# Values of all heads by seven half-size products, five of them in front of head 0, with weight sums and low parts made by accumulating DMAs

## The chip, the core and the metric

One NeuronCore of a Trainium2 chip runs the whole program. The metric is device time in microseconds; the median of the runs counts. PE is TensorE, DVE VectorE, ACT ScalarE, POOL GpSimd, SP the engine that only issues transfers.

## The reference, cut to what matters

A trunk of two layers on 512 tokens of 1024 features. Layer 0 mixes tokens by pooling, layer 1 by differential attention with 8 heads; each is followed by a SwiGLU network, and each sum by a layer norm. The change is in the attention, whose values are one product of (512 x 1024) by (1024 x 1024):

```python
qkv = x @ w_qkv
q, k, v = jnp.split(qkv, 3, axis=-1)
...
s = jnp.einsum('bhcqd,bhckd->bhcqk', q[:, :, :, q0:kend], k[:, :, :, :kend]).astype(jnp.float32) * sm_scale
...
p = jax.nn.softmax(s, axis=-1)
a = p[:, :, 0] - lam * p[:, :, 1]
outs.append(jnp.einsum('bhqk,bhkv->bhqv', a.astype(v.dtype), v[:, :, :kend]))
...
o = o * lax.rsqrt(jnp.mean(jnp.square(o), axis=-1, keepdims=True) + LN_EPS)
```

## The kernel before

Every float32 operand is split into two float32r parts: a high part, which ACT makes by a cast, and a low part, source minus high, which DVE (or POOL) makes by a subtraction. `mm3` (L125) multiplies high by high, high by low and low by high into one bank of PSUM, so each product costs three matmuls. There are eight banks of 128 x 512.

All weights lie in `wall`, in rows of 128 x 1024 (512 KB) in the order of their use. `fetch` lets SP load the next row into one of five raw buffers (`RAWS`), `ready` splits the next row into one of six pairs (`WBUFS`), `take` in the attention gives out the next pairs. A load waits until the buffer five rows back is free. The order of instructions on each engine is the order of the program text: nothing is rearranged, and an instruction that waits holds back all that stand behind it on its engine.

`xt` holds x transposed and split, in two halves of 256 tokens. `transposed` (L210) lets PE turn a block of 128 tokens into two banks, `turned` (L219) lets ACT apply gamma and beta from there, and splits the result into `xt`. Blocks are called 0 to 3. At the end of the first SwiGLU network block 2 is turned in `ffn`, and block 3 by `late` in the middle of head 0.

Attention, for each head h, in this order on PE: the values (two heads of 128 columns are made together for two blocks of tokens, 48 matmuls of 256 columns for each h), the sum of squares of head h-2 (`root`), the queries (24 matmuls of 512 columns), the ten transposes of the weights of head h-1, the keys (24), `mix` of head h-1 with the values (12), and the scores of head h in four blocks (24). Behind the scores DVE adds the bias and takes the row minimum, ACT makes the exponentials, DVE combines the two maps (`combine`); behind `mix` ACT squares and casts (sq, sqh), POOL makes the low part (sql), which `root` multiplies by ones. In heads 1 to 4 DVE also applies gamma and beta to one block of the residual (`affine`). The bias of the next head is loaded by SP one head ahead. Head 0 has no values of an earlier head to mix: its queries and keys are made in two halves of tokens, 96 matmuls of 256 columns, because block 3 is late.

The down projection of `ffn` already uses seven products in place of eight (`DOWN`, `multiply`, L886): two halves of tokens, two halves of the inner dimension, two halves of the columns. There sums of weight quarters are made by accumulating DMAs that POOL issues (`load_terms`, L664 to 666).

Of the kernel before, what the change touches and what calls it, by code (L numbers as in the profile page):

```python
# [54 lines left out]
def trunk(ctx, tc, x, wall, pscale, lam_p, subln, table, lng, lnb, band, first, onehot, out):  # L55
# [37 lines left out]
    total = wall.shape[0]  # L93

    def fetch(upto):
        while fetched[0] < min(upto, total):
            c = fetched[0]
            raws[c] = keep.tile([P, 1024], F32, tag="raw", name=f"raw{c}", bufs=RAWS)
            nc.sync.dma_start(out=raws[c], in_=wall[c])
            fetched[0] += 1  # L100
# [11 lines left out]
    def ready(upto, low=None):  # L112
        while divided[0] < min(upto, total):
            c = divided[0]
            fetch(c + RAWS)
            h, l = weight_pair(f"w{c}")
            split(h, l, raws.pop(c), low=low)
            parts[c] = (h, l)
            divided[0] += 1
# [99 lines left out]
    def turned(n, s):  # L219
        for i, pt in enumerate(turns.pop((n, s))):  # L220
            y = keep.tile([P, 4, P], F32, tag="y", name=f"y{n}_{s}_{i}", bufs=2)
# [12 lines left out]
    def turn(n, s):  # L234
        transposed(n, s)
        turned(n, s)

# [225 lines left out]
    def ffn(layer, late):  # L463
# [5 lines left out]
        with tc.tile_pool(name=f"ffn{layer}", bufs=1) as fp:  # L469
# [392 lines left out]
            load_gb(n)  # L862
# [33 lines left out]
            for p in DOWN:  # L896
# [18 lines left out]
                for s in range(2):  # L915
# [15 lines left out]
                    elif p == "Q4":  # L931
# [17 lines left out]
                        if not final:  # L949
                            turn(n, 1 + s)  # L950
                            ready(c1 + FB + 3 + s)
# [3 lines left out]
    def attention(late):  # L955
        n = 2
        with tc.tile_pool(name="attn", bufs=1) as ap:
# [10 lines left out]
            ah = ap.tile([P, AW], F32R, name="ah")  # L968
            al = ap.tile([P, AW], F32R, name="al")
            for t in (ah, al):  # L970
                nc.gpsimd.memset(t[:, :P].bitcast(F32), 0.0)
# [20 lines left out]
            whole = region("heads").rearrange("p (h i t) -> p h i t", h=HEADS, i=2)  # L992
# [11 lines left out]
            vs, vw, qk, soft, outs, mid, biases = {}, {}, {}, {}, {}, {}, {}  # L1004

            started = {}

            def start_values(h, j):
                c, i = h // 2, h % 2
                if c not in vw:  # L1010
                    vw[c] = take(2)
                if j == 0:
                    started[h] = bank(f"v{h}")
                s = 2 * i + j
                for k in range(KB):
                    wh, wl = vw[c][k // 4]
                    o = (k % 4) * 256
                    mm3(
                        started[h][:, j * 256 : (j + 1) * 256],
                        x_at(k, s * P, (s + 1) * P),  # L1020
                        (wh[:, o : o + 256], wl[:, o : o + 256]),
                        k == 0,
                        k == KB - 1,
                    )

            def values(h):
                for j in range(2):
                    if j or h not in started:
                        start_values(h, j)
                vh = ap.tile([P, 2, 256], F32R, tag="vh", name=f"vh{h}", bufs=3)  # L1030
                vl = ap.tile([P, 2, 256], F32R, tag="vl", name=f"vl{h}", bufs=3)
                return vh, vl, started.pop(h)

            def split_values(h, v):
                vh, vl, acc = v
                split(vh.rearrange("p a b -> p (a b)"), vl.rearrange("p a b -> p (a b)"), acc)
                vs[h] = (vh, vl)

            def query(acc, w, lo, hi):
                wh, wl = w  # L1040
                for k in range(KB):
                    mm3(
                        wide(acc, lo, hi),
                        (wh[:, k * P : (k + 1) * P], wl[:, k * P : (k + 1) * P]),
                        x_at(k, lo, hi),
# [4 lines left out]
            def split_query(h, nm, acc):  # L1050
                hh, ll = (slots[6 if nm == "q" else 7][:, i, :] for i in range(2))
# [77 lines left out]
            def mix(h):  # L1129
                vo = (h % 2) * P  # L1130
                acc = bank(f"o{h}")
                for k in range(SB):
                    vh, vl = vs[2 * (h // 2) + k // 2]
# [3 lines left out]
                        (vh[:, k % 2, vo : vo + P], vl[:, k % 2, vo : vo + P]),  # L1137
# [43 lines left out]

            load_bias(0)
            for h in range(HEADS):
                v = values(h)
                if h > 0:
                    combine(h - 1, 3)
                ready(where[0] + 2)
                split_values(h, v)
# [12 lines left out]
                accs = [bank(f"{nm}{h}") for nm in "qk"]  # L1201
                w = take(2)
                if h == 0:
                    query(accs[0], w[0], 0, 256)
                    late()
                    query(accs[1], w[1], 0, 256)
                ready(where[0] + 1)
                query(accs[0], w[0], 256 if h == 0 else 0, 512)
                split_query(h, "q", accs[0])
                if h > 0:  # L1210
                    transposed(h - 1)
                query(accs[1], w[1], 256 if h == 0 else 0, 512)
                if h == 0:
                    split_query(h, "k", accs[1])
                    start_values(1, 0)
                ready(where[0] + 2)
                if h > 0:
                    split_query(h, "k", accs[1])
                ready(where[0] + 3)
                if h > 0:  # L1220
# [12 lines left out]
            combine(HEADS - 1, 3)  # L1233
            ws = take(4)
# [31 lines left out]
    attention(later(1, 3))  # L1266
# [31 lines left out]
def layout(w):  # L1298
# [32 lines left out]
    v = cols(qkv[:, 2 * D :], 256)  # L1331
    v = v.reshape(4, P, 2, 1024).transpose(0, 2, 1, 3)
    for h in range(HEADS):
        if h % 2 == 0:
            pieces.append(v[h // 2])
# [41 lines left out]
```

## Time and profile before

| | us |
|---|---|
| median of three runs | 949.88 (949.42 to 952.01) |
| span of the profiled execution | 947.3 |
| first value matmul of head 0 | 374.2 |
| first scores of head 0 | 395.9 |
| first scores of head 6 | 527.8 |
| end of the last head's scores | 552.4 |

In the rows of a timeline the columns are start, duration, engine, line, operation, output and inputs, form, number, and in brackets the idle time before it and who ended it. The rows of groups give busy time and the mean in ns. The rows of stages give, for each engine, busy time and number of instructions. "DMA to landing" is minimum, median and maximum from the issue to the arrival.

### The profile page before, as it was taken

Reading aid. Unit: us, or ns where it says so; the run is one execution under the profiler, and the core shown is the slowest. Engines: PE = TensorE matmul, PEld = TensorE weight load, DVE = VectorE, ACT = ScalarE, POOL = GpSimd, SP = SyncE. Lnnn points to the kernel's source line nnn. Section 1 sums busy time; section 2 is a strip of 40 time slices with the busy share of each in tenths; the row PEclk is TensorE's granted clock in tenths of the full one; section 3 lists DMA queues with packets and bytes.
Section 4 is the critical chain, followed back from the end, with each engine's and each line's share of the span. In section 5 each row is a group of like instructions: output and inputs, shape, how many; then the busy total and the mean of one; then the engine's idle time right before and its main releaser. Section 6 shows DMA issues by size and latency. Waiting matters only on the chain.

```text
span 947.3 us, 15363 instructions
## 1 busy us (share of the span) xinstructions
PE 934.1 (99%) x5976; PEld 845.7 (89%) x5976; DVE 781.3 (82%) x1149; ACT 490.1 (52%) x788; POOL 108.4 (11%) x133
## 2 busy tenths in 40 slices
PE   9999999999999999999999999999999999999996
PEld 8898899999988888988888888998899999988885
DVE  8859879999988777688777677789779999987778
ACT  6752444555564457655566553833345554564450
POOL 4121121110001101000000000211111110001101
PEclk9999999999999999999999999999999999999998
DMA  9387988885888964333233222396888885878952
GB/s 244 125 266 236 341 269 246 265 261 208 255 255 271 363 219 136 95 89 101 78 123 83 64 90 90 118 324 197 262 266 250 255 272 204 261 249 271 356 171 90
DMA packets 82248, 196.99 MB, mean 208 GB/s; under 512 B 14804, under 2 KB 26324, under 8 KB 82174
## 3 DMA queue, kind: packets, MB, share of 16 engines
q1 hardware_dynamic: 42876, 115.07, 36.9%
q0 software_dynamic: 15520, 46.14, 17.8%
q10 hardware_dynamic: 23778, 34.78, 10.2%
q8 instruction: 47, 0.77, 0.3%
q14 instruction: 27, 0.22, 0.1%
HBM read 159.25 MB, written 36.72 MB: 207 GB/s over the span
## 4 chain that ended last, share of the span: by engine, by line
PE 92%; DVE 4%; ACT 2%; issue 1%; POOL 0%; DVEq 0%; POOLq 0%
PE A L820 17%; PE P L886 13%; PE C L820 9%; PE Q L886 6%; PE B L820 4%; PE g L129 3%; PE u L128 3%; PE u L127 3%; PE u L129 3%; PE g L127 3%; PE g L128 3%; PE s L1085 2%; PE v L127 2%; PE v L128 2%; PE v L129 2%; PE q L128 2%
## 5 line engine op out<-in xcount | busy, mean ns | idle before, releaser
L566 DVE TENSOR_TENSOR raw<-raw,raw 128x1024 f32<-128x1024 f32 x56 | 68.3, 1219 | 0.5
L109 ACT CAST xs<-hid 128x512 fp32r<-128x512 f32 (+1 forms) x60 | 34.7, 581 | 24.4 <-DVE hid L734 24.4
L224 ACT ACTIVATE y<-pt,bT,gT 128x128 f32<-128x128 f32 x96 | 36.1, 456 | 20.1 <-PE pt L213 20.1
L110 DVE TENSOR_TENSOR xs<-hid,xs 128x512 fp32r<-128x512 f32 (+1 forms) x60 | 38.5, 644 | 7.8 <-ACT xs L109 7.8
L1095 ACT ACTIVATE p<-p,mn 128x128 f32<-128x128 f32 (+3 forms) x64 | 35.4, 554 | 14.9 <-DVE mn L1090 14.9
L665 POOL DMA_DIRECT2D b<-in_wall x20 | 14.0, 705 | 175.0 <-DVE g_58l L572 66.1
L598 DVE TENSOR_TENSOR hid<-sg,u 128x512 f32<-128x512 f32 x16 | 11.0, 687 | 27.5 <-PE u L129 16.8
L726 POOL DMA_DIRECT2D xs<-ssum x24 | 17.4, 725 | 140.7 <-PE Q L886 119.5
L177 POOL TENSOR_TENSOR rs<-rs,mhalf 128x1 f32<-128x1 f32 x16 | 12.5, 784 | 170.5 <-DVE rs L176 131.0
L110 DVE TENSOR_TENSOR xt<-y,xt 128x512 fp32r<-128x512 f32 x24 | 16.3, 689 | 17.5 <-ACT xt L109 17.5
L1090 DVE CUSTOM_DVE_ANT_0 p<-s,bias 128x128 f32<-128x128 f32 (+3 forms) x64 | 28.1, 485 | 0.0
L665 POOL DMA_DIRECT2D hid<-in_wall x24 | 18.7, 821 | 81.1 <-DMA tsum<-hid 49.4
L110 POOL TENSOR_TENSOR sql<-sq,sqh 128x512 fp32r<-128x512 f32 x7 | 9.0, 1291 | 165.3 <-ACT sqh L109 165.3
L702 ACT CAST v<-u 128x512 fp32r<-128x512 f32 x22 | 13.6, 620 | 26.9 <-DVE u L700 26.7
L168 DVE BATCH_NORM_STATS2 st<-res 128x6 f32<-128x512 f32 x32 | 22.2, 695 | 1.1
L846 ACT ACTIVATE sg<-sg 128x512 f32<-128x512 f32 x14 | 8.9, 633 | 25.7 <-DVE sg L839 25.7
L110 DVE TENSOR_TENSOR heads<-k,heads 128x512 fp32r<-128x512 f32 x8 | 5.5, 692 | 19.9 <-ACT heads L109 19.9
L614 ACT CAST xs<-hid 128x1024 fp32r<-128x1024 f32 x8 | 8.4, 1051 | 24.0 <-DVE hid L631 11.6
L666 POOL DMA_DIRECT2D hid<-in_wall x12 | 14.8, 1232 | 48.2 <-DMA hid<-in_wall 44.9
L835 DVE TENSOR_TENSOR hid<-C,hid 128x512 f32<-128x512 f32 x14 | 9.7, 692 | 10.8 <-PE C L820 9.2
L1109 DVE SCALAR_TENSOR_TENSOR p<-p,sm,p 128x128 f32<-128x128 f32 (+3 forms) x32 | 17.7, 552 | 1.1
L109 ACT CAST heads<-k 128x512 fp32r<-128x512 f32 x8 | 4.7, 589 | 26.0 <-PE k L129 26.0
(1119 smaller groups left out, 3727.7 us busy)
## 6 DMA issues: line engine op xcount, KB each, us to landing
raw<-in_wall SPq DMA_DIRECT2D x122, 512.0 KB, 4.5
r<-tsum SPq DMA_DIRECT2D x40, 512.0 KB, 4.3
hid<-in_wall POOLq DMA_DIRECT2D x36, 512.0 KB, 6.9
b<-in_wall POOLq DMA_DIRECT2D x30, 512.0 KB, 6.4
r<-in_wall SPq DMA_DIRECT2D x30, 512.0 KB, 4.5
tsum<-hid ACTq DMA_DIRECT2D x24, 512.0 KB, 5.3
ssum<-v ACTq DMA_DIRECT2D x22, 512.0 KB, 4.4
tsum<-b ACTq DMA_DIRECT2D x20, 512.0 KB, 5.2
```

The costliest lines, as they stand in the source:

```text
L109: nc.scalar.copy(dst_h, src)
L110: (low or nc.vector).tensor_tensor(dst_l, src, dst_h.bitcast(F32), op=ALU.subtract)
L127: nc.tensor.matmul(acc, ah, bh, start=start, stop=False)
L128: nc.tensor.matmul(acc, ah, bl, start=False, stop=False)
L129: nc.tensor.matmul(acc, al, bh, start=False, stop=stop)
L224: nc.scalar.activation(y[:, k, :], pt[:, k * P : (k + 1) * P], AF.Identity, bias=bT[:, n, kk : kk + 1], scale=gT[:, n, kk : kk + 1],)
L566: tt(t, raws[pair[0]], raws[pair[1]], op=ALU.add)
L665: nc.gpsimd.dma_start(out=t[:, j], in_=src[:, j])
L820: nc.tensor.matmul(o, w[:, c], x[:, kk, :], start=p in ("P1", "Q5", "P2") and f + kk + e == 0, stop=p in ("Q4", "Q3", "P2") and (f, kk, e) ...
L886: nc.tensor.matmul(accs[s], x[:, k, r], y[:, c], start=first and k == 0 and e == 0, stop=last and k == m - 1 and e == 2, skip_group_check= ...
L1090: nc.vector.tensor_tensor_reduce(out=p, in0=accs[c][:, :w], in1=biases[h][:, w - 1 :: -1] if w < S else biases[h][:, ::-1], op0=ALU.add, o ...
L1095: nc.scalar.activation(p, p, AF.Exp, bias=mn[:, q, c : c + 1], scale=-1.0, accum_out=sm[:, q, c : c + 1],)
```

## The change

The value weights are cut into quarters W11, W12, W22, W21 (first index: half of the inner dimension, second: half of the columns, two rows of `wall` each), and x into X11, X12 (tokens 0 to 255) and X21, X22. Seven products of (256 x 512) by (512 x 512) take the place of eight: P1 = X11 W11, P2 = X12 W21, P6, P7, Q4, Q5 and Q3 with sums of quarters on the left, on the right or on both. All values of all heads are kept in float32 in `vals` (16 KB per partition), and each head splits its 128 columns from there.

Five products (P1, P2, P6, P7, Q4) stand in front of head 0, with the queries and keys of head 0 (now 48 matmuls of 512 columns) between P2 and P6; Q5 and Q3 are in head 1. Heads 2 to 7 make no values. Blocks 2 and 3 are both turned in the attention, and their float32 form is kept (`kept`) for the sums over x, which DVE and ACT make as in `ffn`.

The right-hand sums are made by accumulating DMAs on POOL's queue: `tall` (in the place of gamma and beta, which are loaded later) is W11, then plus W12, plus W22, and after its first use plus W21; `short` is W12 plus W22; rows 6 and 7 are W11 plus W12 in the raw buffer. For 14 rows of queries and keys (8, 9 and 12 to 23 counted from the attention's first row) the low part is no longer a subtraction on DVE: ACT casts the high part, ACT writes its negative into the low part, and a DMA adds the row from memory to it.

```diff
+    order_of_rows = (
+        [vrow[0], vrow[0] + 1, vrow[3], vrow[3] + 1, qrow, qrow + 1, vrow[0], vrow[0] + 1]
+        + [qrow + 2, qrow + 3, vrow[2], vrow[2] + 1]
+        + list(range(qrow + 4, qrow + 2 * HEADS))
+    )
...
+    added = {attn + 6 + r: vrow[1] + r for r in range(2)}
+    by_dma = {attn + c for c in (8, 9, *range(12, 24))}
...
-            nc.sync.dma_start(out=raws[c], in_=wall[c])
+            nc.sync.dma_start(out=raws[c], in_=wall[rows_of_wall[c]])
+            if c in added:
+                nc.gpsimd.dma_start(out=raws[c], in_=wall[added[c]], accum_op=ALU.add)
...
+            if c in by_dma:
+                nc.scalar.copy(h, raw)
+                nc.scalar.mul(l, raw, -1.0)
+                nc.gpsimd.dma_start(
+                    out=l, in_=wall[rows_of_wall[c]].bitcast(F32R), accum_op=ALU.add
+                )
+            else:
+                split(h, l, raw, low=low)
...
+            nc.sync.dma_start(out=tall, in_=two_rows(0))
+            nc.sync.dma_start(out=short, in_=two_rows(1))
+            nc.gpsimd.dma_start(out=tall, in_=two_rows(1), accum_op=ALU.add)
+            nc.gpsimd.dma_start(out=short, in_=two_rows(2), accum_op=ALU.add)
+            nc.gpsimd.dma_start(out=tall, in_=two_rows(2), accum_op=ALU.add)
...
+            def values(p, r, accs, w):
+                wh, wl = w
+                xh, xl = (lefts[p][:, i] for i in range(2))
+                for s in range(2):
+                    t = slice(s * P, (s + 1) * P)
+                    for q in range(2):
+                        kk = 2 * r + q
+                        c = slice(q * 512, (q + 1) * 512)
+                        for e, (a, b) in enumerate(((xh, wh), (xh, wl), (xl, wh))):
+                            nc.tensor.matmul(
+                                accs[s], a[:, kk, t], b[:, c],
+                                start=p in ("P1", "Q5", "P2") and kk + e == 0,
...
+            flip(1, 2)
+            va = [bank(f"va{s}") for s in range(2)]
+            w = take(2)
+            for r in range(2):
+                values("P1", r, va, w[r])
+            flipped(1, 2, (r0, r1))
+            whole_x(r2, 0, 0)
+            flip(1, 3)
+            ready(where[0] + 3)
+            vb = [bank(f"vb{s}") for s in range(2)]
+            w = take(2)
+            for r in range(2):
+                values("P2", r, vb, w[r])
+            whole_x(r3, 0, 1)
+            flipped(1, 3, (r0, r1))
+            ready(where[0] + 2)
+            combined(r1, r0, r1, ALU.subtract)
+            combined(r0, r2, r0, ALU.subtract)
+            combined(r2, r1, r2, ALU.subtract)
+            accs = [bank(f"{nm}0") for nm in "qk"]
+            w = take(2)
+            query(accs[0], w[0])
+            high(3, r0)
+            high(0, r2)
+            for s in range(2):
+                nc.scalar.copy(part(0, 0, s), vb[s])
+            low(3, r0)
+            low(0, r2)
+            wide6 = [pair_of(f"vt{r}", tall[:, r]) for r in range(2)]
+            nc.gpsimd.dma_start(out=tall, in_=two_rows(3), accum_op=ALU.add)
+            for s in range(2):
+                combined(part(0, 0, s), va[s], part(0, 0, s), ALU.add)
+            split_query(0, "q", accs[0])
+            query(accs[1], w[1])
+            wide7 = [pair_of(f"vs{r}", short[:, r]) for r in range(2)]
+            for r in range(2):
+                values("P6", r, va, wide6[r])
+            split_query(0, "k", accs[1])
+            for s in range(2):
+                nc.scalar.copy(part(0, 1, s), va[s])
+            combined(r3, r3, r2, ALU.add)
+            high(1, r1)
+            high(2, r3)
+            for r in range(2):
+                values("P7", r, va, wide7[r])
+            low(1, r1)
+            wide4 = [pair_of(f"vu{r}", tall[:, r]) for r in range(2)]
+            for s in range(2):
+                nc.scalar.copy(part(1, 1, s), va[s])
+            low(2, r3)
+            load_gb(1)
+            for r in range(2):
+                values("Q4", r, va, wide4[r])
+            ready(where[0] + 4)
...
             load_bias(0)
             for h in range(HEADS):
-                v = values(h)
                 if h > 0:
                     combine(h - 1, 3)
-                ready(where[0] + 2)
-                split_values(h, v)
+                if h == 1:
+                    vc = [bank(f"vc{s}") for s in range(2)]
+                    w = take(2)
+                    for r in range(2):
+                        values("Q5", r, vc, w[r])
+                    ready(where[0] + 4)
+                    for s in range(2):
+                        combined(part(1, 1, s), vc[s], part(1, 1, s), ALU.subtract)
+                if h > 0:
+                    split_values(h - 1)
                 if h > 1:
                     root(h - 2)
...
+                    query(accs[1], w[1])
+                    ready(where[0] + 2)
                     split_query(h, "k", accs[1])
+                    if h == 1:
+                        w = take(2)
+                        for r in range(2):
+                            values("Q3", r, vc, w[r])
...
+                    ready(where[0] + 3)
                     mix(h - 1)
```

More of the change, by code (lines that the diff above doesn't have):

```diff
@@ L236, in turn @@
         turned(n, s)
+    flip, flipped = transposed, turned
     lines = dram.tile([HEADS, LINE], F32, name="lines")
@@ L1026, in values @@
[L1026 to L1036, printed above, removed]
+            vs, qk, soft, outs, mid, biases = {}, {}, {}, {}, {}, {}
@@ L1265, in trunk @@
     ffn(0, {(0, 1): later(0, 2), (1, 0): later(0, 3)})
-    attention(later(1, 3))
+    attention()
     ffn(1, {(0, 1): later(2, 3)})
```

148 lines of the change are left out of this document (90 added, 58 removed).

## The prediction

> **What bounds the kernel now.** I read the page's engine line, TensorE's waits, then busy time by stage.
>
> ```profile
> span 947.3 us, 15363 instructions
> PE 934.1 (99%) x5976; PEld 845.7 (89%) x5976; DVE 781.3 (82%) x1149; ACT 490.1 (52%) x788; POOL 108.4 (11%) x133
> PE q L128 <- DVE xt L110: 0.2, 1, 0.2
> 373.40:395.86 22.46, 22.29 (x184) 21.96 (x184) 13.76 (x25) 16.42 (x31) 1.00 (x4) 1.00 0.34 101
> 491.21:513.70 22.49, 22.49 (x145) 19.79 (x144) 15.13 (x39) 13.32 (x31) 1.29 (x1) 1.00 0.29 84
> ```
>
> The page gives PE 99%, and of the waits of all PE's matmuls the only one inside attention is the 0.2 us on xt. The two stage rows (from the first transpose of block 2 to the first scores; from the q of one head to the q of the next; columns PE, PEld, DVE, ACT, POOL, then granted clock) say that PE has no idle time there to give back, while ACT is busy 13.32 us and DVE 15.13 us of 22.49. So fewer matmul columns are worth their time, if nothing new makes PE wait; and a new wait costs its full length.
>
> **The saving.** First and last matmul of groups of 24 (256 and 512 columns), the instruction behind each, and twelve 512-column matmuls of the kind that the products will be (x stationary):
>
> ```profile
> 380.07 0.28 PE L127 MATMUL q<-xt,w70h 128*128 128x256 f32 x1
> 382.83 0.29 PE L129 MATMUL q<-xt,w70l 128*128 128x256 f32 x1
> 382.96 1.03 PE L213 MATMUL pt<-ident,res 128*128 128x128 f32 x8
> 383.75 0.36 PE L127 MATMUL k<-xt,w71h 128*128 128x256 f32 x1
> 491.21 0.40 PE L127 MATMUL q<-xt,w84h 128*128 128x512 f32 x1
> 496.66 1.25 PE L1120 MATMUL at<-ident,p 128*128 128x128 f32 x10
> 301.89 0.39 PE L886 MATMUL P<-d_14h,xs 128*128 128x512 f32 x1
> 304.61 0.39 PE L886 MATMUL P<-d_15h,xs 128*128 128x512 f32 x1
> ```
>
> 256 columns take (382.96-380.07)/24 = 0.120 us, 512 take 5.45/24 = 0.227, for x stationary 2.72/12 = 0.227. Values: 8 heads x 48 x 0.120 = 46.1 us now; 7 products x 24 x 0.227 = 38.1 after. Head 0's queries and keys: 96 x 0.120 = 11.5 becomes 48 x 0.227 = 10.9. **Saving 8.6 us**, all on the path. Transposes stay.
>
> **Front: weight sums against PE.** P6 needs W11, W12 and W22 added by two accumulating DMAs onto one tile, 1 MB each, one after the other. Rows: the SP queue, landings of the loads, of plain and of accumulating POOL loads (512 KB each), the best throughput, and one cast, subtraction and evacuation each:
>
> ```profile
> 373.40 1.09 PE L213 MATMUL pt<-ident,res 128*128 128x128 f32 x8 [0.16 <-DVE res L186]
> 375.85 0.33 SPq L99 DMA_DIRECT2D raw<-in_wall  x1
> 376.99 0.42 SPq L964 DMA_DIRECT2D gcol<-in_subln  x1
> 377.45 0.43 SPq L1058 DMA_DIRECT2D bias<-lines  x1
> DMA to landing us min/median/max: 3.5/4.2/4.9
> L665 POOL DMA_DIRECT2D hid<-in_wall x24: 722/739/1240, 46.4 to 744.2; - x24
> DMA to landing us min/median/max: 4.2/6.4/10.5
> L666 POOL DMA_DIRECT2D hid<-in_wall x12: 1222/1230/1243, 55.1 to 748.6; - x12
> DMA to landing us min/median/max: 5.8/6.9/10.8
> 22.00:24.00 2.00, 2.00 (x19) 2.00 (x18) 1.97 (x5) 0.00 (x0) 0.56 (x1) 1.00 1.04 426
> L109 ACT CAST w70h<-raw x1: 1042/1042/1042, 373.5 to 373.5; 128x1024 fp32r<-128x1024 f32 x1
> L110 DVE TENSOR_TENSOR w70l<-raw,w70h x1: 1226/1226/1226, 374.6 to 374.6; 128x1024 fp32r<-128x1024 f32 x1
> L110 DVE TENSOR_TENSOR vl<-v,vh 128x512 fp32r<-128x512 f32 x8 | 5.5, 684 | 0.0
> ```
>
> 512 KB at 426 GB/s is 1.2 us of data. Accumulating lands 1.6 later than plain at the least (5.8 against 4.2), so its data part is 2.8. No row shows 1 MB accumulating: I take 5.8+2.8 = 8.6; bounds below. The tile's first load takes the place of the bias load on SP, 377.45, and lands 4.2+1.2 later: 382.8. Two accumulations: 400.0. Then cast 1.04, two subtractions 2x1.23, and P1's sum must be read out of the bank that P6 goes on adding to (0.7): P6 can start at 404.2. PE gets there at 373.40 + 2x0.79 (transposes) + 4x5.45 (P1, P2, q, k) = 396.8. **Wait 7.4.** Low end: a megabyte at the price of 512 KB, 5.8: 1.8. High end: the accumulation onto the other tile stands between the two on POOL, and its 5.6 of data runs in front of the second by 2.5: 9.9. The accumulation of raw row 7 is ahead of them on POOL: it waits for SP's load of 375.85, 4.2 later 380.0, and takes 1.23, so it is through 1.5 us before the tile lands; if that cover goes, the wait grows by the same.
>
> One rule speaks against the change here. The Trainium skill ("SBUF — State Buffer", "Who interferes with whom") has DVE and GpSimd share a port pair that one locks for a whole instruction; POOL's descriptors can be held by DVE. Here plain issues of POOL took 739 ns in the median and 1240 at most beside a DVE that is 82% busy, so three issues could lose 1.5 us by these rows, 3.7 if each waited for one subtraction; I add nothing.
>
> Queued behind ACT's waiting cast are the split of head 0's q, the second half of the sum, the other tile's casts and k's split; PE asks for none of them before P7 or the scores. The sums over x (10 x 1.23 on DVE, 4 x 1.04 on ACT) I cost at nothing: P2, q and k hide them. Block 3's activations and splits lie in these rows, first and last:
>
> ```profile
> 383.59 1.51 ACT L224 ACTIVATE y<-pt,bT,gT 128x128 f32<-128x128 f32 x4 [0.75 <-PE pt L213]
> 387.85 0.69 DVE L110 TENSOR_TENSOR xt<-y,xt 128x512 fp32r<-128x512 f32 x1 [1.37 <-ACT xt L109]
> ```
>
> They took 5.0 us (to 388.54). Now the transposes end at 373.40+2x0.79+5.45 = 380.4, so 386.5 with one row split between, and five steps of 1.2 lead to the low half that P6 reads: 392.5, 4 us before PE. With that cover gone each further step costs 1.2.
>
> **Head 0's bias.** Its load stood at 377.45, 18 us early. Now it is on SP behind the gamma and beta load (held until the fourth sum of weights is split) and four raw loads, the last of which needs the buffer of row 8, free after two casts, a copy and a copy with the sign turned on ACT, 4 x 1.0, begun about with Q4.
>
> ```profile
> bias<-lines SPq DMA_DIRECT2D x8, 256.0 KB, 3.5
> ```
>
> Landing at Q4 start + 4.0 + 0.7 (issues) + 3.5 = 8.2, or up to 3.7 later for three of the loads. Q4 and the scores take 5.45+2.1; Q5 then needs banks that the scores fill until a first minimum (0.5): wait 1.1 to 4.8. I take 3.0; ends 0 (loads drained early) and 5.
>
> **Heads 2 to 7: less to cover with.** Before, 48 value matmuls (5.8 us) stood between the scores of a head and the sum of squares of the last. Scores 6 on PE, ACT, POOL, DVE:
>
> ```profile
> 526.42 1.05 ACT L109 CAST w92h<-raw 128x1024 fp32r<-128x1024 f32 x1
> 527.92 0.60 ACT L1145 ACTIVATE sq<-o 128x512 f32<-128x512 f32 x1 [0.45 <-PE o L129]
> 528.55 0.62 ACT L109 CAST sqh<-sq 128x512 fp32r<-128x512 f32 x1
> 529.25 1.29 POOL L110 TENSOR_TENSOR sql<-sq,sqh 128x512 fp32r<-128x512 f32 x1 [21.21 <-ACT sqh L109]
> 527.75 2.21 PE L1085 MATMUL s<-heads 64*128 64x256 f32 x24
> 529.89 0.38 PE L127 MATMUL v<-w86h,xt 128*128 128x256 f32 x1
> 536.18 0.75 DVE L1109 SCALAR_TENSOR_TENSOR p<-p,sm,p 128x512 f32<-128x512 f32 x1
> L205 DVE TENSOR_TENSOR res<-res,gb 128x1024 f32<-128x1024 f32 x8 | 9.8, 1219 | 0.0
> 490.98 0.40 PE L1153 MATMUL ss<-sql,ones 128*128 128x512 f32 x1
> ```
>
> sql ends at 530.54; PE is free at 529.89, and without values its next matmul reads sql: 0.65 of wait even in today's order. The row of weights behind k now takes two ACT passes instead of one: 1.0 more against 0.45 idle ahead of sq, so 0.6 later: **1.2 per head**. Second, the transposes need the last combination, done at 536.93 (+0.5 for the same ACT delay). PE reaches the one that needs it at 529.89 + 1.2 + 0.46 (ss) + 5.45 (q) + 0.3 = 537.3, so it hides most of this: 0.2 more. Six heads: 8.4. Floor: ACT not late, 0.7 each, 4.2. In heads 2 to 4 DVE also has the affine of one block (2 x 1.22) ahead of scaled and the q and a splits, with 5.8 us less to do it in; DVE's 15.13 less three row subtractions plus 2.4 is 13.9 of 16.7, in order, behind ACT: I estimate 1.2 per head, 3.6 (0 to 7.2). **Together 12.0** (4.2 to 15.6). The 14 subtractions taken from DVE (17 us) shorten nothing that PE waits for; the low parts that DMA completes are asked for 12 us later, against 5.8 to 6.9 of landing.
>
> Moving the gamma and beta load, raw sums of rows 6 and 7 and the reordered rows change no PE work; they were loaded a head early.
>
> **Sum.** -8.6 + 7.4 + 3.0 + 12.0 = +13.8: span 961.1. The median of the runs shown is 949.88, 2.6 above the span, so **963.7**. The ends: -8.6+1.8+0+4.2 = -2.6, 947.3; -8.6+9.9+5+15.6 = +21.9, 971.8.
>
> **Rivals.** (1) *The heads keep pace*, the other side: one mechanism, at the wait for sql and the last combination. If PE comes there no earlier than these (below 0.1 us a head), the 12.0 fall away: 951.7, no change. For it: the first minimum of scores 6 waited for a row subtraction that is gone. Against: 530.54 against 529.89, with today's ACT. (2) *The weight sums come early*, 5.8 a megabyte: 5.6 less, 958.1. (3) *All is hidden* but that 1.8: -6.8, 943.1; it needs both and the bias in time. (4) *The front is worse*: wait 9.9, and the clock falls in it, P6's 5.45 at half speed: 963.7+2.5+5.5 = 971.7.
>
> ```profile
> 935.00:940.00 5.00, 3.57 (x16) 2.63 (x14) 4.97 (x9) 0.00 (x0) 0.05 (x1) 1.00 0.39 145
> 940.00:947.00 7.00, 0.00 (x0) 0.00 (x0) 3.62 (x7) 0.00 (x0) 0.92 (x1) 0.56 0.33 123
> ```
>
> For (4): where PE stands still at the end, the granted clock is 0.56. The Trainium skill ("TensorE: Matmul & The Clock Gate", "Part 1: The HAM clock gate") says that a window of some 3.4 us idle halves the clock, and as long a busy one restores it: an estimate by that page is 1.7 us after a wait like P6's, in place of 5.5. No row in the middle of this kernel shows such a wait.
>
> **Numbers.** Forecast 0.52, (1) 0.14, (2) 0.14, (3) 0.12, (4) 0.08. A measurement tells 0.3% (2.8 us) from no change: faster is (3) and 0.02 of (1), 0.14; same 0.07 of (1); slower the rest, 0.79. Range 947 to 973, from the low end of the sum to just past (4): only (3) and some of (4) lie outside. The forecast alone: 957 to 970.
>
> **What would show it.** PE idle of 2 to 10 us at the first matmul of P6, released by DVE's reading of P1's banks, ACT's cast before it waiting for a DMA; PE idle at Q5 from minima that wait for the bias; in heads 2 to 7 PE idle of about 1 us at ss, released by POOL's sql; a head then lasts 18 to 20 us, not 22.5. Wrong if P6 follows k without a gap, or if ss follows the scores without one: then DMA or ACT is faster in place than the rows say.

## The result, and the profile after

| | before | after |
|---|---|---|
| median, us | 949.65 (949.25 to 952.01) | 980.50 (979.31 to 981.94) |
| span of the profiled execution, us | 947.3 | 979.3 |
| first scores of head 0 | 395.9 | 431.5 |
| first scores of head 1 | 415.2 | 471.5 |
| first scores of head 7 | 550.3 | 582.1 |

The ratio is 1.0325 (95% interval 1.0308 to 1.0342). The forecast was 963.7, its range ended at 973: the direction is right, the time is 16.8 us off. After the first scores of head 7 both kernels need the same, 397.0 and 397.2 us of span, so all of the loss lies in the attention ahead of it.

The engine line of the page after, columns as before:

```profile
span 979.3 us, 14929 instructions
PE 935.2 (96%) x5712; PEld 831.6 (85%) x5712; DVE 786.3 (80%) x1157; ACT 515.7 (53%) x820; POOL 127.3 (13%) x153
```

PE has 264 matmuls fewer and is yet busy 1.1 us longer, and its idle time grew from 13.2 to 44.1 us. Two causes show in the next two views: waits, and a lower clock. First the waits of PE's matmuls (engine, line, tile, who ended the wait; us in total, times, longest):

```profile
PE va L1067 <- DVE vals L1246: 15.1, 1, 15.1
PE vc L1067 <- DVE mn L1140: 9.8, 1, 9.8
PE ss L1202 <- POOL sql L124: 3.3, 6, 0.9
PE q L151 <- DMA w80l<-in_wall: 1.2, 1, 1.2
```

Before, the list had 0.2 us inside the attention. The first row is P6 waiting until DVE has read P1's sums, the second Q5 waiting until DVE's first minima free the banks of the scores. Then busy time by stage (PE, PEld, DVE, ACT, POOL, granted clock, DMA share, GB/s): from the transposes to the end of k, the wait, P6 in two pieces, the wait at Q5, Q5:

```profile
373.19:397.00 23.81, 23.79 (x112) 19.61 (x112) 18.86 (x22) 15.20 (x29) 4.43 (x6) 1.00 0.97 258
397.00:412.09 15.09, 0.00 (x0) 0.03 (x1) 3.11 (x4) 4.18 (x5) 1.63 (x2) 0.64 0.64 125
412.09:417.60 5.51, 5.51 (x13) 4.35 (x14) 5.05 (x6) 0.67 (x2) 0.74 (x1) 0.50 0.76 132
417.60:423.00 5.40, 5.40 (x24) 4.38 (x24) 0.75 (x1) 2.91 (x4) 0.00 (x0) 0.95 0.30 60
434.43:444.25 9.82, 0.00 (x1) 0.00 (x1) 0.63 (x5) 0.51 (x3) 0.00 (x0) 0.72 1.04 297
444.25:450.00 5.75, 5.75 (x16) 4.57 (x17) 5.49 (x23) 4.42 (x15) 0.00 (x0) 0.60 0.08 33
```

In the first stage PE is never idle, as forecast, but look at the DMA share: 0.97 of all sixteen DMA engines. In the kernel before it was 0.34 up to the first scores (a row of the prediction), and the forecast never added up what the change puts on top of that. After the wait PE runs at clock 0.50 for 5.5 us and does 13 matmuls where 24 would fit. P6 took 412.09 to 420.48, 8.4 us, in place of 5.45, and Q5 7.75: 2.9 and 2.3 us that are no wait in any list.

Where the 15.1 us come from, in the rows of the timeline around the weight sums (start, duration, engine, line, operation, what ended the idle time):

```profile
377.58 0.38 SPq L1004 DMA_DIRECT2D tall<-in_wall  x1
385.01 1.21 POOL L1006 DMA_DIRECT2D tall<-in_wall  x1 [3.02 <-DMA tall<-in_wall]
389.89 1.20 POOL L1007 DMA_DIRECT2D vals<-in_wall  x1 [3.67 <-DMA vals<-in_wall]
398.56 1.18 POOL L1008 DMA_DIRECT2D tall<-in_wall  x1 [7.48 <-DMA tall<-in_wall]
407.91 1.04 ACT L123 CAST vt0h<-tall 128x1024 fp32r<-128x1024 f32 x1 [15.17 <-DMA tall<-in_wall]
411.26 1.28 DVE L1246 TENSOR_TENSOR vals<-va,vals 128x512 f32<-128x512 f32 x2
412.09 0.77 PE L1067 MATMUL va<-vt0h,heads 128*128 128x512 f32 x1 [15.11 <-DVE vals L1246]
```

The chain is the forecast one, link by link: load, first accumulation, second accumulation, cast, DVE, P6. Its durations are not: the load took 7.4 us (forecast 5.4), the first accumulation 13.5 (8.6), the second 9.3 (8.6). The other tile, whose load stands behind it on SP and whose accumulation stands between on POOL, is in `vals` (that is where `short` lies).

What the DMA engines of the kernel after did from 376 to 410 us (queue, packets, MB, share of 16 engines; then issues with KB each and median us to landing):

```profile
q0 software_dynamic: 1042, 3.94, 58.8%
q1 hardware_dynamic: 1264, 3.80, 31.8%
...
tall<-in_wall POOLq DMA_DIRECT2D x2, 1024.0 KB, 11.2
...
vals<-in_wall POOLq DMA_DIRECT2D x1, 1024.0 KB, 13.1
```

The same two queues over the whole span of the kernel before:

```profile
q1 hardware_dynamic: 42876, 115.07, 36.9%
q0 software_dynamic: 15520, 46.14, 17.8%
```

0.588 x 34 us for 3.94 MB is 5.1 us of all sixteen engines per MB on POOL's queue, which carries the accumulations here; 0.318 x 34 for 3.80 MB is 2.8 us per MB on SP's queue of plain loads. Together that is 30.8 of 34 us, and the last sum that P6 needs is there at 407.9: until then the engines are full, and what is queued on them needs about the time that passes. Accumulating costs nearly twice the engine time of plain loading. The page of before had a hint: 0.178 x 947.3 / 46.14 = 3.65 us per MB on POOL's queue, where some transfers accumulate, against 3.04 on SP's. At those prices the same 3.94 and 3.80 MB make 25.9 us. Counted from 376, that estimate has the last sum at 402 and a wait of about 9 us at P6: nearer than the forecast, and still short.

The wait at Q5, rows of the timeline:

```profile
426.53 0.33 SPq L177 DMA_DIRECT2D gb<-in_lng  x1
...
431.06 1.01 SPq L1108 DMA_DIRECT2D bias<-lines  x2
...
443.89 0.29 DVE L1140 CUSTOM_DVE_ANT_0 p<-s,bias 128x128 f32<-128x128 f32 x1 [8.65 <-DMA bias<-lines]
444.25 0.80 PE L1067 MATMUL vc<-w74h,heads 128*128 128x512 f32 x1 [9.82 <-DVE mn L1140]
```

The bias is issued 5.1 us after Q4 began (forecast 4.7) and is read 12.8 us later (landing forecast at 3.5, at most 7.2): gamma and beta, four rows of weights and two low parts are on the same engines, whose share in the wait is 1.04.

The heads. Score to score (start of the first scores of heads 1 to 7) six heads took 582.1 - 471.5 = 110.6 us; PE's own work in them is 6 x (22.5 - 5.8) = 100.2, so they lose 10.4. Four rows of PE, from the scores of head 3 to the queries of head 4, show of what:

```profile
508.98 2.08 PE L1135 MATMUL s<-heads 64*128 64x256 f32 x22 [0.34 <-DVE heads L124]
511.30 0.50 PE L1201 MATMUL ss<-sqh,ones 128*128 128x512 f32 x1 [0.23 <-ACT sqh L123]
512.65 0.50 PE L1202 MATMUL ss<-sql,ones 128*128 128x512 f32 x1 [0.86 <-POOL sql L124]
512.99 0.39 PE L149 MATMUL q<-xt,w84h 128*128 128x512 f32 x1
```

The scores began at 508.26. From there to the queries PE needs 4.7 us where it has 2.6 of work: it waits for the split of the keys, for ACT's cast and for POOL's low part in turn. These three waits make 1.4 of the 2.1 us lost. The profile books the rest as busy time of the matmuls beside them, so the list of waits understates such a loss, and PE's busy time does not show the work that was saved.

### The profile page after: what moved, and what is told of

The parts are those of the page before. It is cut to its first block, busy times and chain, and to the rows that moved or that the text cites. A ratio compares the mean times of both kernels' runs of the same rounds, so it can differ in the third digit from the quotient of the medians.

```text
span 979.3 us, 14929 instructions
## 1 busy us (share of the span) xinstructions
PE 935.2 (96%) x5712; PEld 831.6 (85%) x5712; DVE 786.3 (80%) x1157; ACT 515.7 (53%) x820; POOL 127.3 (13%) x153
## 4 chain that ended last, share of the span: by engine, by line
PE 40%; DVE 8%; issue 4%; ACT 4%; DMA 2%; POOL 0%; DVEq 0%; SPq 0%; ACTq 0%; POOLq 0%
PE A L847 8%; PE P L914 6%; PE C L847 4%; PE Q L914 3%; PE B L847 2%; PE g L149 2%; PE u L151 2%; PE u L149 2%; PE g L151 2%; PE g L150 2%; PE u L150 1%; PE va L1067 1%; DVE p L1140 1%; DVE p L1159 1%; DVE p L1155 1%
## 5 line engine op out<-in xcount | busy, mean ns | idle before, releaser
L1145 ACT ACTIVATE p<-p,mn 128x128 f32<-128x128 f32 (+3 forms) x64 | 35.3, 553 | 22.5 <-DVE mn L1140 22.5
L249 ACT ACTIVATE y<-pt,bT,gT 128x128 f32<-128x128 f32 x80 | 30.1, 456 | 19.4 <-PE pt L235 19.4
L1140 DVE CUSTOM_DVE_ANT_0 p<-s,bias 128x128 f32<-128x128 f32 (+3 forms) x64 | 28.1, 486 | 13.8 <-DMA bias<-lines 8.7
L692 POOL DMA_DIRECT2D b<-in_wall x20 | 14.0, 706 | 172.1 <-DVE g_58l L599 65.3
L753 POOL DMA_DIRECT2D xs<-ssum x24 | 17.5, 727 | 141.8 <-PE Q L914 67.9
L625 DVE TENSOR_TENSOR hid<-sg,u 128x512 f32<-128x512 f32 x16 | 11.0, 686 | 27.3 <-PE u L151 16.5
L729 ACT CAST v<-u 128x512 fp32r<-128x512 f32 x22 | 13.6, 620 | 27.4 <-DVE u L727 27.4
L124 DVE TENSOR_TENSOR xt<-y,xt 128x512 fp32r<-128x512 f32 x20 | 13.6, 690 | 13.5 <-ACT xt L123 13.5
L693 POOL DMA_DIRECT2D hid<-in_wall x12 | 14.8, 1234 | 47.9 <-DMA hid<-in_wall 43.7
L1067 PE MATMUL va<-vt0h,heads 128*128 128x512 f32 x8 | 4.6, 645 | 15.1 <-DVE vals L1246 15.1
L862 DVE TENSOR_TENSOR hid<-C,hid 128x512 f32<-128x512 f32 x14 | 9.7, 691 | 10.7 <-PE C L847 9.1
L858 ACT COPY hid<-C 128x512 f32<-128x512 f32 x14 | 8.2, 588 | 18.5 <-PE C L847 18.5
L693 POOL DMA_DIRECT2D b<-in_wall x10 | 12.3, 1233 | 37.6 <-DMA b<-in_wall 37.6
```

The costliest lines, as they stand in the source:

```text
L124: (low or nc.vector).tensor_tensor(dst_l, src, dst_h.bitcast(F32), op=ALU.subtract)
L249: nc.scalar.activation(y[:, k, :], pt[:, k * P : (k + 1) * P], AF.Identity, bias=bT[:, n, kk : kk + 1], scale=gT[:, n, kk : kk + 1],)
L692: nc.gpsimd.dma_start(out=t[:, j], in_=src[:, j])
L1140: nc.vector.tensor_tensor_reduce(out=p, in0=accs[c][:, :w], in1=biases[h][:, w - 1 :: -1] if w < S else biases[h][:, ::-1], op0=ALU.add, o ...
L1145: nc.scalar.activation(p, p, AF.Exp, bias=mn[:, q, c : c + 1], scale=-1.0, accum_out=sm[:, q, c : c + 1],)
```

## The experiments

All of them change the kernel after. The kernel before, run alongside, had medians of 949.3 to 949.6.

**Was the bias late because of its place in the queue?** Head 0's bias loaded ahead of the weight sums, as before the change:

```diff
+            load_bias(0)
             nc.sync.dma_start(out=tall, in_=two_rows(0))
...
-            load_bias(0)
             for h in range(HEADS):
```

> The bias of head 0 is loaded in front of the weight sums instead of behind the gamma and beta load and the raw rows. Theory A (the 16 DMA engines are full at both places, a load is late by what is queued in front of it): the 9.8 us of PE idle at Q5 and the half clock of its first matmuls (2.3 us) go, the bias's 0.65 us of data delays P6 by as much: 980.5 - 9.8 - 2.3 + 0.7 = 969.1. Theory B (the minima of head 0 are late for another reason as well: the table load and the lambda scalars at 435, the banks): the wait shrinks to 3 to 5 us only, 974 to 976.

Measured 972.14 (970.61 to 973.25), 8.4 less. P6 and Q5 in the timeline of this run:

```profile
413.44 0.77 PE L1083 MATMUL va<-vt0h,heads 128*128 128x512 f32 x1 [16.03 <-DVE vals L1249]
436.84 0.50 PE L1083 MATMUL vc<-w74h,heads 128*128 128x512 f32 x1 [1.07 <-DVE mn L1143]
```

Q5's stage, in the same columns as above:

```profile
436.84:442.40 5.56, 5.56 (x24) 4.62 (x25) 5.33 (x22) 4.24 (x15) 0.00 (x0) 1.00 1.05 269
```

8.75 us of wait at Q5 and its half clock are gone. The time lies between the two numbers expected, 3.0 above the first, and the trace has most of this. P6 begins 1.35 us later than in the kernel after, where 0.7 was expected. In head 2 the wait for the low part of w80, a DMA, grew from 1.2 to 1.65 us:

```profile
467.28 0.80 PE L151 MATMUL q<-xt,w80l 128*128 128x512 f32 x1 [1.65 <-DMA w80l<-in_wall]
```

And behind that wait the clock fell once more, to 0.50 from 469 to 470 us: these queries took 8.98 us, wait included. In the kernel after the same queries, with a wait of 1.23, ran at 1.00 and took 6.99: 0.4 us of the difference is the longer wait and 1.6 the clock.

**Is it the order on POOL, or the engines' time?** `short` loaded by POOL behind the first accumulation onto `tall`, and accumulated last, so no other accumulation stands between the two that P6 needs (its load still does):

```diff
-            nc.sync.dma_start(out=short, in_=two_rows(1))
             nc.gpsimd.dma_start(out=tall, in_=two_rows(1), accum_op=ALU.add)
-            nc.gpsimd.dma_start(out=short, in_=two_rows(2), accum_op=ALU.add)
+            nc.gpsimd.dma_start(out=short, in_=two_rows(1))
             nc.gpsimd.dma_start(out=tall, in_=two_rows(2), accum_op=ALU.add)
+            nc.gpsimd.dma_start(out=short, in_=two_rows(2), accum_op=ALU.add)
```

> The 1 MB load of the second weight tile is issued by POOL behind the first accumulation instead of by SP in front of it, its own accumulation last. Theory A (engine time shared with other queues makes the first accumulation 13.5 us long): 2.6 us of other data less beside it, so P6 starts 2 to 4 us earlier, its wait is 11 to 13 us, 976.5 to 978.5. Theory B (the accumulations cost what they cost by issue, landing and POOL's order): no change at P6, 980.5 within 1.

Measured 977.85 (976.54 to 978.36). The wait at P6:

```profile
PE va L1067 <- DVE vals L1246: 11.2, 1, 11.2
```

3.9 us off the wait, not all of it. The first accumulation took 10.7 us in place of 13.5 (issued 385.37, the second at 396.04), with the load of the other tile no longer ahead of it: 2.9. The second, now ahead of the other tile's accumulation, took 8.2 in place of 9.3 (ACT's cast at 404.27): 1.1. So less came from the order among the accumulations than from what else was on the engines. How long the two would take on idle engines no run shows.

**What do the low parts by DMA cost?**

```diff
-    by_dma = {attn + c for c in (8, 9, *range(12, 24))}
+    by_dma = set()
```

> All rows of queries and keys are split by ACT and DVE again; ACT makes one pass per row instead of two and 14 accumulations go. Theory A: two accumulations of 2.6 us of engine time no longer share the engines with the bias: wait at Q5 about 5 in place of 9.8; ACT reaches sq earlier, the waits for the sums of squares shrink by half, 2 us: 972 to 974. Theory B (the low parts by DMA were needed to relieve DVE, which has 16.7 us a head now): DVE gets 2.4 us a head back and PE waits for it in heads 2 to 4: the heads get longer by 3 us or more, the gain at Q5 is used up, 979 or above.

Measured 971.74 (970.59 to 972.35), 8.8 less. The waits of PE:

```profile
PE va L1067 <- DVE vals L1246: 15.5, 1, 15.5
PE vc L1067 <- DVE mn L1140: 5.2, 1, 5.2
...
PE at L1170 <- DVE p L1159: 1.1, 3, 0.4
```

4.6 us of the 9.8 at Q5 were the two low parts that shared the engines with the bias, though the bias was issued 0.9 us later here than in the kernel after. In the kernel after POOL's queue, which carried these two, took 52.5% of the engines' time from 434 to 444 us, 5.25 us. The six heads take 106.7 in place of 110.6: 1.2 us of that is the wait for w80's low part, the rest lies where PE waited for sql (3.3 us in all, now 0.4), because without ACT's second pass sq, sqh and sql come earlier. DVE, given back its 14 subtractions, is late by 0.4 at the most. The DMA route was a loss in both places.

**Does PE's standing still cause the half clock?** Work that nobody reads put into the wait, first 10.9 us, then 13.6:

```diff
             query(accs[1], w[1])
+            spare = bank("spare")
+            for _ in range(2):
+                query(spare, w[1])
...
```

> PE makes the keys of head 0 twice more into a spare bank (10.9 us of matmuls that nobody reads) in the wait in front of P6; nothing else is changed. Clock theory: the granted clock stays at 1.0 through P6, which takes 5.5 instead of 8.4 us; the wait for the weight sums ends when it did: 980.5 - 2.9 = 977.6. Rival (P6 is slow because its operands come late, not by the clock): P6 takes 8.4 again, 980.5.

> Computation added: the queries' product with head 0's key weights is made two and a half times more into a bank that nobody reads, 60 matmuls, 13.6 us of PE's wait before P6. If the slow P6 and P7 come from PE standing still, P6 then takes 5.45 to 6 us in place of 8.4, and the time falls by up to 2.9 to 977.6 us (976.5 to 979). Rival: the clock falls for another reason (the wait of about 1 us that is left, or the load of all engines), P6 stays over 7.5 us and the time is 980 to 981.5.

The first gave 981.72 (980.66 to 982.48), no gain, the second 978.92 (977.46 to 979.32). The stages of the first (wait left, P6):

```profile
408.00:412.02 4.02, 0.27 (x2) 0.03 (x1) 3.10 (x4) 4.02 (x5) 0.45 (x1) 0.87 0.00 0
412.02:418.00 5.98, 5.98 (x14) 4.68 (x15) 5.05 (x6) 0.67 (x2) 0.74 (x1) 0.51 0.77 136
```

and of the second, first the matmul that begins P6, then P6 as a stage:

```profile
412.80 0.47 PE L1067 MATMUL va<-vt0h,heads 128*128 128x512 f32 x1 [1.28 <-DVE vals L1246]
```

```profile
412.80:418.25 5.45, 5.45 (x24) 4.51 (x25) 5.05 (x6) 1.26 (x3) 0.73 (x1) 1.00 0.78 132
```

The first was expected at 977.6 and missed it; the second came near. The miss is itself the measurement: 3.8 us of idle time were enough to halve the clock for the next 6 us, 1.3 us were not (nor 1.07 at Q5 in the run with the early bias). With DVE, DMA and the matmuls of P6 the same, it is PE's idle time that does it. Its price here: P6 8.4 instead of 5.45. Between these two the length of the wait alone does not decide: 1.65 us halved the clock in the run with the early bias, and 2.1 us left it at 1.00 in heads 3 and 4 of a run below (gamma and beta on POOL), while head 2 of that run fell to 0.50 with waits of the same lengths. What decides there stays open.

**Are the sums late only because they are asked for late?** `tall` loaded and accumulated while the down projection runs, where gamma and beta were loaded before (the load was issued at 267.2 us, 110 us earlier, not the 35 of the expectation):

```diff
+                talls.append(keep.tile([P, 2, D], F32, tag="gb", name="tall"))
+                nc.sync.dma_start(out=talls[0], in_=two_rows(0))
+                for c in (1, 2):
+                    nc.gpsimd.dma_start(out=talls[0], in_=two_rows(c), accum_op=ALU.add)
...
```

> Same work as the changed kernel; only the first load of tall and its two accumulations are issued about 35 us earlier, before the down projection of the first SwiGLU network, where gamma and beta were loaded before. If the 15.1 us in front of P6 are the queueing of these transfers among all that is under way from 376 to 407 us, P6 follows k with less than 1 us of wait, its half clock (2.9 us) goes too, and the time is 980.5 - 15.1 - 2.9 = 962.5 us (961 to 965); the wait at Q5 stays at 8 to 10 us. Rival: the transfers only push the others, the other tile and the products P7 and Q4 or the down projection are late in turn: 966 us or more, with a new wait in front of P7 or in the down projection.

Measured 965.58 (963.57 to 966.64), 14.9 less. The first accumulation still took 12.1 us there (issued 274.98, the second at 287.12), beside a DMA share of 0.91, but nothing waits for it. P6 has no wait at all:

```profile
399.20 0.47 PE L1071 MATMUL va<-vt0h,heads 128*128 128x512 f32 x1
```

Of the 3 us over the number expected, 2.4 lie ahead of P1, which begins at 376.43 in place of 374.04; but that start moves by about 1 us from execution to execution (375.0 in the run with 13.6 us of filler, whose code is the same up to there), so how much of it is the added traffic stays open. 0.8 us of it is a wait at 306.4, in the down projection, for a cast of ACT; the kernel after has no such wait.

**Do the parts add up?** `tall` early, bias early and no low parts by DMA, together; and the same with the sum of squares behind the queries:

```diff
-                if h > 1:
-                    root(h - 2)
...
                     query(accs[0], w[0])
+                    if h > 1:
+                        root(h - 2)
                     split_query(h, "q", accs[0])
```

> Three parts of the change undone together: tall early as in the first of these runs, head 0's bias early, and all low parts by subtraction on DVE again. If the waits are additive, 15.1 + 2.9 at P6, 9.8 + 2.3 at Q5 and about 1.5 of the heads' go: 980.5 - 31.6 = 949 us (947 to 953), no wait over 2 us in front of P6 or Q5, and the heads still 17.5 to 18 us each. Rival: the waits cover one another, and one of over 4 us appears elsewhere (P7, Q4, the first scores): 955 us or more.

> As the run before, and the sum of squares of head h-2 is put behind the queries of head h in place of in front of them. If the 1 us that PE waits there in each of six heads is the low part of POOL coming 0.65 us or more too late for a place straight behind the scores, this takes 3 to 6 us off: 943 to 946 us. Rival: the transposes behind the queries then wait for the last combination of the maps instead (it ends no earlier), and the time stays within 1 us of the run before.

Measured 948.86 (947.56 to 949.59; ratio to before 0.9982 to 1.0001) and 949.28 (948.29 to 950.71). The first is the expected 949: the parts add up. Undone together they take off 31.6 us, all of the change's loss of 30.9 and 0.7 more, which is no measurable gain over the kernel before. The second gained nothing. PE's rows of the first, from the scores of head 4 to the queries of head 6:

```profile
496.68 2.30 PE L1142 MATMUL s<-heads 64*128 64x256 f32 x22 [0.21 <-DVE heads L124]
...
505.82 0.98 PE L1177 MATMUL at<-ident,p 128*128 128x128 f32 x7 [0.39 <-DVE p L1166]
...
516.98 0.50 PE L1209 MATMUL ss<-sql,ones 128*128 128x512 f32 x1 [0.21 <-POOL sql L124]
```

Small waits for DVE's split, for DVE's combination and for POOL, in one head or the next. Moving `root` took the last one away, and the transposes waited that much longer for the combination (2.6 us over six heads in place of 1.2 over three). The delays are longer than these waits. From the start of one group to the start of the next, in head 3 of the first run, the scores take 2.84 us (2.13 in the kernel before) and the transposes 1.60 (1.01); behind the scores of head 5 the two matmuls of the sum of squares take 1.04 (0.46) and the transposes 1.32. These three places make up what is lost, 0.9 to 1.4 us a head.

**Can the heads be had for less?** Four tries on the last of these kernels. One: a row's subtraction moved on DVE from in front of the first minimum to behind the split of the values. Two: that, and gamma and beta applied by POOL. Three: the transposes behind the first three key matmuls, with one low part a head by DMA. Four: behind six.

```diff
+                if h > 1:
+                    ready(where[0] + 3)
...
-                    ready(where[0] + 3)
+                    if h in (1, HEADS - 1):
+                        ready(where[0] + 3)
```

```diff
-        nc.vector.tensor_tensor(z, z, gb[:, 0, :], op=ALU.mult)
-        nc.vector.tensor_tensor(z, z, gb[:, 1, :], op=ALU.add)
+        nc.gpsimd.tensor_tensor(z, z, gb[:, 0, :], op=ALU.mult)
+        nc.gpsimd.tensor_tensor(z, z, gb[:, 1, :], op=ALU.add)
```

```diff
+    by_dma = {attn + c for c in range(15, 24, 2)}
...
+                    query(accs[1], w[1], range(1))
                     transposed(h - 1)
-                    query(accs[1], w[1])
+                    query(accs[1], w[1], range(1, KB))
```

> As the run with the sum of squares behind the queries, and in heads 2 to 6 the subtraction of the second row of weights stands on DVE behind the split of the values, where DVE waits for the queries, in place of between the split of the keys and the first minimum. If what is left of the heads' 1.3 us each is that DVE reaches the first minimum late (514.96 us where the scores begin at 514.06, 497.59 where they begin at 495.93), the chain to the last combination moves forward by 0.5 us in heads 5 and 6 and up to 1.2 in heads 2 to 4: 2 to 4 us less than that run, 945 to 947 us. Rival: in heads 2 to 4 DVE is full (16.95 us busy of 18.0) and only the order changes: less than 1 us.

> As the run before it, and gamma and beta of the residual in heads 1 to 4 are applied by POOL in place of DVE (2.4 us of DVE a head). If DVE's load is the bound of heads 2 to 4, they come down from 18.1 to about 17 us: 2 to 4 us less than the run before it, 942 to 945 us, below the kernel before by 0.5 to 0.8%. Rival: POOL's passes of some 2.5 us each slow DVE down or delay the low part that the sum of squares needs, and the time is the same or up to 3 us more.

> As the run with everything early and the sum of squares behind the queries, with two edits in the heads. The transposes stand behind the first three of the 24 key matmuls (0.7 us later on PE), and the low part of one of two rows of weights a head, the one split ahead of the keys, is completed by DMA again in heads 2 to 6, where ACT has 1.2 us idle for the second pass. If what is left are the 0.3 to 0.8 us at the transposes (last combination late) and the 0.7 us at the scores (DVE's split of the keys behind the row's subtraction), some 1.0 us a head goes: 947.0 - 5 = 942 us of span, median 944 (942.5 to 946.5), 0.3 to 0.7% below the kernel before. Rival: the next link of the same chain (split of the transposes, then mix) waits in its place, and the time stays within 1 us of 949.

> As the run before it, with the transposes behind six of the 24 key matmuls in place of three. If the last combination is still late by up to 0.3 us there, this takes up to 1 us more off. Rival: the split of the transposes is then late for mix (it ended 1.0 us ahead in heads 5 and 6), and the time is 1 to 3 us more than with three.

None of the four gained what was expected; in one and three the rival named beforehand came true:

| | median, us | first scores, head 1 to head 7 | six heads |
|---|---|---|---|
| three parts undone | 948.86 | 442.5 to 549.2 | 106.7 |
| and root later | 949.28 | 442.2 to 549.1 | 106.9 |
| one: subtraction moved | 949.52 | 441.7 to 549.5 | 107.8 |
| two: affine on POOL | 964.33 | 447.9 to 563.6 | 115.7 |
| three: transposes later | 949.44 | 442.6 to 550.1 | 107.5 |
| four: still later | 950.12 | 443.6 to 551.0 | 107.4 |

One, three and four take their own wait away, or half of it (one: 2.6 to 1.4 us at the transposes), and find it again one link on: in three, the last two of the six intervals fall from 17.5 to 17.1 us, but the two from head 2 to head 4 rise from 18.1 to 18.7, where mix now takes 2.8 us in place of 2.0. The 6 to 7 us that are left sit in no single place; whether another order of the whole head would give them back was not tried.

Two shows something else. POOL and DVE behind the scores of head 3 of that run, and the same DVE lines behind the scores of head 4 in the run named one, without POOL beside them:

```profile
493.18 2.40 POOL L227 TENSOR_TENSOR res<-res,gb 128x1024 f32<-128x1024 f32 x1
493.34 2.39 DVE L1166 SCALAR_TENSOR_TENSOR p<-p,sm,p 128x128 f32<-128x128 f32 x1
495.65 0.55 DVE L1147 CUSTOM_DVE_ANT_0 p<-s,bias 128x384 f32<-128x384 f32 x1
495.65 2.40 POOL L228 TENSOR_TENSOR res<-res,gb 128x1024 f32<-128x1024 f32 x1
...
496.80 1.41 DVE L1162 TENSOR_SCALAR p<-p,sm,nlam 128x256 f32<-128x256 f32 x1
```

```profile
499.80 0.35 DVE L1166 SCALAR_TENSOR_TENSOR p<-p,sm,p 128x128 f32<-128x128 f32 x1
...
501.21 0.41 DVE L1162 TENSOR_SCALAR p<-p,sm,nlam 128x256 f32<-128x256 f32 x1
```

DVE's instruction of 0.35 us lasts until POOL's ends, 2.39; the minimum from PSUM at 495.65, begun in the same moment as POOL's next, takes its usual 0.55. The Trainium skill ("SBUF — State Buffer", "Who interferes with whom") says this: a DVE instruction with two SBUF inputs, or in a two-port mode, and a GpSimd instruction that reads SBUF exclude each other for a whole instruction. Here the trace agrees, with 2.0 and 1.0 us lost in these two rows; for POOL's DMA issues in the changed kernel (0.9 to 1.2 us) the prediction added nothing, and no run here shows a loss by them.

## Why the prediction was right or wrong

- **The saving, 8.6: right.** P1, P2 and head 0's queries and keys take 5.4 to 5.6 us each in the trace, and P6, P7 and Q4 16.5 together in the run with `tall` early, where nothing is late. With the three parts undone: -8.6 + 6.5 for the heads (106.7 - 100.2) + 0.5 in the scores of head 0 + 1.2 of a later start of P1 = -0.4; the span is 946.9 against 947.3.
- **The wait at P6, 7.4 (1.8 to 9.9): the mechanism right, the size wrong, 15.1.** This is the first failing step: "512 KB at 426 GB/s is 1.2 us of data ... so its data part is 2.8", and from it 8.6 a megabyte with one neighbour added. A landing time measured on a queue with room says what one transfer needs, not what thirty microseconds of queued traffic leave to it. The two rows of raw sums, the loads of both tiles, the rows of weights and three accumulations share sixteen engines that are 97% busy. The links that follow the last landing were right (4.2 us from there to P6, as forecast). The runs showed the rest twice: reordering POOL's queue gained 3.9 of 15.1, starting early all of it.
- **Head 0's bias, 3.0 (0 to 5): the place right, the size wrong, 9.8.** The same error: the issue was forecast to 0.4 us, and then 3.5 us of landing taken from a quiet queue. 12.8 was the price; loading it early took 8.75 of the wait away.
- **The low parts by DMA at nothing: wrong.** "... the low parts that DMA completes are asked for 12 us later, against 5.8 to 6.9 of landing" looked at their own landing. That was 6.3 to 10.6 us here, and w80's low part was waited for, 1.2 us. The larger cost came through others: 4.6 us of the bias's wait. In the heads undoing them gained 3.9; 1.2 of it is w80's wait, and the other 2.7 goes with ACT's second pass in front of sq, which the forecast did count, at 0.6 a head.
- **The clock at nothing: wrong, 5.2.** Rival (4) had it at 5.5 for P6 alone; it came as 2.9 and 2.3, at two places. The Trainium skill ("TensorE: Matmul & The Clock Gate", "Part 1: The HAM clock gate") gave an estimate of 1.7 for each, from 3.4 us of slow running. The traces fit neither half of it, and they decide. Waits of 3.8 us and more halved the clock at P6 and Q5, but 1.65 us did it too in the run with the early bias. And the half speed lasted 3.3 us there, 4.7 at Q5 and 6 at P6, at a price of 1.6, 2.3 and 2.9.
- **Heads 2 to 7, 12.0: right, 10.4.** Behind the scores of head 3 the two matmuls of the sum of squares take 1.69 us in place of 0.46, so 1.2 as forecast, and 0.9 more is lost to the split of the keys, where DVE had been estimated at 1.2. That the total comes so near is in part luck: it holds the 1.2 of w80's low part, which the forecast had at nothing.
- **Rival (1), heads that keep pace: refuted**; even with these three parts undone they lose 6.5. **(2) and (3)** fell with the queue. **(4)**, 971.7, was the nearest, and too small.

The sum over again, with what was measured: -8.6 + 15.1 + 9.8 + 5.2 + 10.4 = 31.9, and the span grew by 32.0; forecast were 13.8. The forecast's step from span to time, 2.6, compared the median with one execution: the profiled execution of the kernel after took 981.04 for a span of 979.3, 1.7 more.

## What to carry to other kernels

Price a transfer on a busy stretch by engine time: all bytes queued there times us per MB from the queue table (share x span / MB), not by the landing time of a lone one. Here an accumulated MB took 5.1 us where a plain one took 2.8, and prices from the page of before still came out at 25.9 of 30.8. Ask for an operand built in steps by DMA so early that nothing waits for it, even 100 us ahead, if a buffer allows it. An algorithm that saves 8.6 us of PE in a kernel whose PE is 99% busy also removes cover, and the engines behind it, each late by half a microsecond, ate 6.5 of it here.

## What the runs showed of the hardware that was not expected

- Accumulating DMA: 5.1 us of all sixteen engines per MB on the queue that carried it, 2.8 for plain loads beside it.
- The clock: 3.8 us without a matmul halved it for 6 us (0.51), 1.07 and 1.28 us left it at 1.00; in between 1.65 us halved it once, and 2.1 us did so in one head and not in two others.
- POOL at elementwise work in SBUF stretched DVE's combination from 0.35 to 2.39 us, while minima read from PSUM kept their 0.55; moving 2.4 us of DVE work a head to POOL cost 14.8 us in all (964.33 against 949.52).
